# RWKV slots moved and the 16x16 inversion rewritten in a hybrid recurrent decoder layer

## The chip, the cores and the metric

One core of a Trainium2 chip runs the whole step. The metric is device time in microseconds (us), as the median of several executions. The engines are TensorE (PE in the profile), VectorE (DVE), ScalarE (ACT), GpSimd (POOL) and the DMA queue of SyncE (SP); each works through its own queue of instructions in order, and they meet at semaphores.

## The reference, cut to what matters

One layer with three parallel branches (HGRN2, RWKV-7, a short gated convolution) on 256 prompt tokens and 8 x 8 sample tokens, merged by sigmoid gates, then an MLP. The change touches the RWKV branch alone. Per head (16 heads of 64 channels), token after token:

```python
def step(S, inp):                       # S: [value, key]
    r_, w_, k_, v_, kk_, a_ = inp
    sa = jnp.einsum('bhij,bhj->bhi', S, -kk_)
    S = (S * w_[:, :, None, :] + sa[..., None] * (kk_ * a_)[:, :, None, :]
         + v_[..., None] * k_[:, :, None, :])
    return S, jnp.einsum('bhij,bhj->bhi', S, r_)
...
o_rw = (o_rw + bonus.reshape(Bn, T, RW_WIDTH)) * g      # after a group norm; g = sigmoid(gd) @ rw_g2
y_b = o_rw @ w_pb
```

The kernel does this in chunks of 64 tokens (four of the prompt, one that holds the 64 sample tokens). Within a chunk the tokens depend on one another through a strictly triangular 64x64 matrix N per head, and the kernel needs the inverse of (1 - N).

## The kernel before, in words

**Stages.** First a short prologue (about 30 us), then the RWKV stage with the convolution (about 30 to 545 us), then HGRN2 with the first merge, two more merges, the output projection, and the MLP. Each large product is split into two float32r parts, three matmuls for one: a weight granule `raw` of 128x1024 comes by DMA (line 128), ScalarE rounds it to `whi_t` (line 120), VectorE writes the rest `wlo_t` (line 121), and TensorE runs lines 147 to 149.

**Slots.** The order of TensorE's queue in the RWKV stage is written out by hand: a loop over slots, and in each some steps of dense projections (8 of 128x320 for each granule), with steps of the five chains `front`, `sample`, `chunk`, `solve` and `tail` between them. Heads go in pairs, eight pairs (0 to 7), 12 slots apart. A tuple says in which slots after its start a pair's chain makes its next step: `FRONT = (-7, -6, -3, 0, 1, 2)`, `SOLVE = (0, 2, 9, 15, ...)`, `CHUNK = 21 to 32`, `TAIL = (33, 39, 40)`. The other engines' queues are put in order by a scheduler with its own estimate of time and by priorities, so a change of cost or place there moves other instructions too.

**A pair's way.** The dense steps give its tiles k, r and v; `shift_mix` mixes each with the token before (POOL: `Rk` or `Rr`, then `Rd` at line 351; DVE: `xsk`, `xsr`, `xsv` at line 353).

- `front` step 1: squares on ScalarE (466), sums on TensorE (469), a reciprocal root. Step 2: two small products `lora` (489), ScalarE's sigmoids and exponential, POOL's `sg` (499), DVE's scan `Wp` (501), `W`, and its reciprocal `Wi` (505). Step 3: transposes (512), then `kkn` (516), `LYR` (522, 523 on DVE, 524, 525 on POOL), `a` times `Wi` on POOL (530), and `BK` (529, 531 on DVE, 532 on ScalarE).
- `solve` step 1 (line 592): products of `BK` and `LYR` into `pi`, masked into `Nb`. Step 2: the sample chunk's; then `Nb` goes to DRAM (616), its forty diagonal 16x16 blocks (five chunks, two heads, four each) come back as 40 partitions of 256 numbers, `Nd` (621), are inverted into `Pd`, are stored (649), and the whole comes back as `Pm` (651). From slot 15 on TensorE joins the 16x16 inverses to 32 and 64 (672 to 685).
- `chunk`: per chunk of 64 tokens three steps, each of them a product that needs what the step before left in `X` or `Y` (line 730 and, for the sample, 785 copy `X` on DVE; 725 makes `Sw` on POOL).
- `tail`: group norm, and as its last step the gate product (848) and its use (850).

**The inversion before**, all on VectorE: inside each 4x4 block by substitution (lines 631, 633), then twice joined, 4 to 8 and 8 to 16, by products that are written out as a multiplication into `t1` (638) and a sum over it (640).

Of the kernel before, what the change touches and what calls it, by code (L numbers as in the profile page):

```python
# [9 lines left out]
F32 = mybir.dt.float32  # L10
# [3 lines left out]
ALU = mybir.AluOpType  # L14
# [76 lines left out]
NSLOT = 12  # L91
URGENT = 1000

FRONT = (-7, -6, -3, 0, 1, 2)
SOLVE = (0, 2, 9, 15, 16, 17, 18, 19, 20)
SAMPLE = (20, 21, 22, 23)

CONV = (3, 0, 1, 1, 1, 1, 1, 0)
CHUNK = tuple(range(21, 33))
TAIL = (33, 39, 40)  # L100


class K:
# [252 lines left out]
    def rwkv(self, cx):  # L356
# [43 lines left out]
        blocks = (50 - len(self.early)) * 16  # L400
        chains = ((front, FRONT), (sample, SAMPLE), (chunk, CHUNK), (solve, SOLVE), (tail, TAIL))
        total = 8 * NSLOT + TAIL[-1] + 1
        with self.tc.manual_schedule(engines={mybir.EngineType.PE}):
# [168 lines left out]
    def rwkv_solve(self, j, wp):  # L572
        nc, io = self.nc, self.io
        V, G, S, T = nc.vector, nc.gpsimd, nc.scalar, nc.tensor
# [8 lines left out]
        for mk, cc in (("mkp", slice(0, 4)), ("mks", slice(4, 5))):  # L583
            n = cc.stop - cc.start
# [9 lines left out]
            for h, rows in ((0, lo), (1, hi)):  # L594
# [4 lines left out]
                m = self.cst(mk)  # L599
# [11 lines left out]
        def blocks(d, c):  # L611
            v = d.rearrange("(b w) -> b w", w=_DG)[:, 0:16 * 640]
            return v.rearrange("b (s x) -> b s x", x=640)[:, :, c * 128:c * 128 + 16]
        dN, dP = self.dN[j % 2], self.dP[j % 2]
        flat = lambda d: d[0:128 * 640].rearrange("(p x) -> p x", x=640)
        nc.sync.dma_start(flat(dN), Z["Nb%d" % (j % 2)])
        Nf = wp.tile([40, 272], F32, name="Nd")
        Pf = wp.tile([40, 272], F32, name="Pd")
        Nd, Pd = (t[:, 0:256].rearrange("p (s t) -> p s t", t=16) for t in (Nf, Pf))
        for c in range(5):  # L620
            nc.sync.dma_start(Nd[8 * c:8 * c + 8], blocks(dN, c))
        S.copy(Pf[:, 0:256], self.cst("eye16")[0:40])

        dg = lambda t: t.rearrange("p (b x) -> p b x", x=68)[:, :, 0:64].rearrange(
            "p b (s t) -> p b s t", t=16)[:, :, :, 0:4]
        N4, P4 = dg(Nf), dg(Pf)
        t1 = wp.tile([40, 512], F32, name="t1")
        for u in (3, 2, 1):
            w = 4 - u
            t4 = t1[:, 0:4 * u * w].rearrange("p (b s t) -> p b s t", b=4, t=w)  # L630
            V.tensor_mul(t4, N4[:, :, 0:u, u:u + 1].to_broadcast([40, 4, u, w]),
                         P4[:, :, u:u + 1, u:4].to_broadcast([40, 4, u, w]))
            V.tensor_add(P4[:, :, 0:u, u:4], P4[:, :, 0:u, u:4], t4)

        def product(out, x, y, n):

            t3 = t1[:, 0:n * n * n].rearrange("p (s t u) -> p s t u", t=n, u=n)
            V.tensor_mul(t3, x.unsqueeze(2).to_broadcast([40, n, n, n]),
                         y.rearrange("p u t -> p t u").unsqueeze(1).to_broadcast([40, n, n, n]))
            V.tensor_reduce(out, t3, axis=mybir.AxisListType.X, op=ALU.add)  # L640
        np_ = wp.tile([40, 64], F32, name="np")
        for n in (4, 8):
            for o in range(0, 16, 2 * n):
                a, b = slice(o, o + n), slice(o + n, o + 2 * n)
                m = np_[:, 0:n * n].rearrange("p (s t) -> p s t", t=n)
                product(m, Nd[:, a, b], Pd[:, b, b], n)
                product(Pd[:, a, b], Pd[:, a, a], m, n)
        for c in range(5):
            nc.sync.dma_start(blocks(dP, c), Pd[8 * c:8 * c + 8])
        yield  # L650
# [755 lines left out]
```

## Time and profile before

| | |
|---|---|
| median of 3 runs | 2437.85 us (2435.94 to 2445.15) |
| profiled execution | 2436.21 us, span 2434.4 us |
| busy: PE, PEld, DVE, ACT, POOL | 98%, 95%, 59%, 39%, 15% |
| mean granted TensorE clock | 0.993 |
| RWKV stage, 180 to 240 us (60 us): PE, DVE, ACT, POOL busy | 57.42, 54.66, 31.02, 17.83 us |
| MLP, 1600 to 2380 us (780 us): PE, DVE, ACT, POOL busy | 780.00, 391.89, 264.90, 7.94 us |

The span runs from the first to the last instruction of one execution. Matmuls are pipelined, so a busy PE is not PE at its peak. In the MLP TensorE never waits; in the RWKV stage it does, and VectorE is nearly as busy as it is. A row of a timeline is: start, duration, engine, line, operation, tiles written and read, shape, and in brackets the idle time of the engine before it with what ended that.

### The profile page before, as it was taken

The numbers are of one execution on the slowest core, as the hardware profiler recorded it, in microseconds if no ns is written. First come the engines' busy times: TensorE is split into PE (matmuls) and PEld (weight loads), VectorE is DVE, ScalarE is ACT, GpSimd is POOL, SyncE is SP. The second block draws the span as 40 slices with busy tenths as digits, with TensorE's granted clock in tenths as the row PEclk, the third lists the DMA queues.
The fourth block names the chain that finished last, engine by engine and source line by source line (L and its number), as shares of the span: only waits on it lengthen the run. The fifth ranks groups of instructions, "written<-read, shape, count | busy, mean of one in ns | idle before, by whom it ended". The sixth has DMA issues, their size and how long they took to land.

```text
span 2434.4 us, 40742 instructions
## 1 busy us (share of the span) xinstructions
PE 2384.3 (98%) x16190; PEld 2317.6 (95%) x16190; DVE 1441.4 (59%) x2485; ACT 961.3 (39%) x1467; POOL 362.1 (15%) x494
## 2 busy tenths in 40 slices
PE   8899999999999999999999999999999999999998
PEld 8899998999999999999999897999999999999996
DVE  6879898666566555644555336644555545554545
ACT  6445444334444444433433335333333333333333
POOL 4423332121111111100000442200000000000003
PEclk9999999999999999999999999999999999999999
DMA  6433434345434443444444744444444444444443
GB/s 224 121 122 113 112 124 129 124 141 183 138 137 140 141 141 127 144 150 147 150 154 147 246 177 153 153 153 151 147 150 153 147 149 152 150 147 152 152 147 130
DMA packets 136877, 360.23 MB, mean 148 GB/s; under 512 B 35440, under 2 KB 48112, under 8 KB 136688
## 3 DMA queue, kind: packets, MB, share of 16 engines
q1 hardware_dynamic: 136688, 357.63, 43.2%
q8 instruction: 128, 2.10, 0.3%
q14 instruction: 61, 0.50, 0.1%
HBM read 339.82 MB, written 17.76 MB: 147 GB/s over the span
## 4 chain that ended last, share of the span: by engine, by line
PE 89%; DVE 6%; ACT 2%; POOL 1%; issue 1%; DMA 1%; SPq 0%; DVEq 0%; POOLq 0%; ACTq 0%
PE mm_t L147 27%; PE mm_t L148 27%; PE mm_t L149 26%; DVE wlo_t L121 1%; PE plv_t L1025 1%; PE pho_t L1075 1%; ACT whi_t L120 1%; PE pi L677 1%; PE pi L592 0%; PE pi L684 0%; PE wide_t L1146 0%; PE wide_t L1147 0%; PE wide_t L866 0%; DVE m L1333 0%; DVE Wi L505 0%
## 5 line engine op out<-in xcount | busy, mean ns | idle before, releaser
L120 ACT CAST whi_t<-raw 128x1024 fp32r<-128x1024 f32 (+1 forms) x600 | 625.2, 1043 | 1137.2 <-PE mm_t L148 984.3
L121 DVE TENSOR_TENSOR wlo_t<-raw,whi_t 128x1024 fp32r<-128x1024 f32 (+1 forms) x600 | 764.8, 1276 | 433.3 <-ACT whi_t L120 431.9
L147 PE MATMUL mm_t<-xh,whi_t 128*128 128x320 f32 x2048 | 648.7, 317 | 0.0
L148 PE MATMUL mm_t<-xl,whi_t 128*128 128x320 f32 x2048 | 635.5, 310 | 0.0
L149 PE MATMUL mm_t<-xh,wlo_t 128*128 128x320 f32 x2048 | 634.8, 310 | 0.0
L147 PEld LDWEIGHTS mm_t<-xh,whi_t 128*128 128x128 f32 x2048 | 386.2, 189 | 7.6 <-issue 4.0
L148 PEld LDWEIGHTS mm_t<-xl,whi_t 128*128 128x128 f32 x2048 | 386.4, 189 | 1.1
L149 PEld LDWEIGHTS mm_t<-xh,wlo_t 128*128 128x128 f32 x2048 | 385.9, 188 | 0.0
L147 PE MATMUL mm_t<-hh,whi_t 128*128 128x320 f32 x1232 | 381.1, 309 | 0.0
L149 PE MATMUL mm_t<-hh,wlo_t 128*128 128x320 f32 x1232 | 380.4, 309 | 0.0
L148 PE MATMUL mm_t<-hl,whi_t 128*128 128x320 f32 x1232 | 380.4, 309 | 0.0
L147 PE MATMUL mm_t<-rh,whi_t 128*128 128x320 f32 x1024 | 316.4, 309 | 0.0
L149 PE MATMUL mm_t<-rh,wlo_t 128*128 128x320 f32 x1024 | 316.4, 309 | 0.0
L148 PE MATMUL mm_t<-rl,whi_t 128*128 128x320 f32 x1024 | 316.4, 309 | 0.0
L147 PEld LDWEIGHTS mm_t<-hh,whi_t 128*128 128x128 f32 x1232 | 231.1, 188 | 6.5 <-ACT whi_t L120 6.5
L148 PEld LDWEIGHTS mm_t<-hl,whi_t 128*128 128x128 f32 x1232 | 231.1, 188 | 0.0
L149 PEld LDWEIGHTS mm_t<-hh,wlo_t 128*128 128x128 f32 x1232 | 231.1, 188 | 0.0
L147 PEld LDWEIGHTS mm_t<-rh,whi_t 128*128 128x128 f32 x1024 | 192.2, 188 | 0.0
L148 PEld LDWEIGHTS mm_t<-rl,whi_t 128*128 128x128 f32 x1024 | 192.2, 188 | 0.0
L149 PEld LDWEIGHTS mm_t<-rh,wlo_t 128*128 128x128 f32 x1024 | 192.2, 188 | 0.0
L1308 DVE TENSOR_TENSOR m<-m,mm_t 128x320 f32<-128x320 f32 x112 | 54.6, 487 | 152.3 <-PE mm_t L149 152.3
L1238 POOL TENSOR_TENSOR ssf<-ssf,sqt 128x320 f32<-128x320 f32 x14 | 19.5, 1396 | 834.8 <-ACT sqt L1237 834.8
(423 smaller groups left out, 2716.7 us busy)
## 6 DMA issues: line engine op xcount, KB each, us to landing
raw<-w_in SPq DMA_DIRECT2D x256, 512.0 KB
raw<-w_ff SPq DMA_DIRECT2D x256, 512.0 KB
raw<-w_o SPq DMA_DIRECT2D x32, 512.0 KB
hs<-s_hg SPq DMA_DIRECT2D x16, 512.0 KB
raw<-w_pc SPq DMA_DIRECT2D x16, 512.0 KB
raw<-w_pb SPq DMA_DIRECT2D x16, 512.0 KB
raw<-w_pa SPq DMA_DIRECT2D x16, 512.0 KB
o_hgs<-hsn SPq DMA_DIRECT2D x16, 256.0 KB
```

The lines of the kernel that those rows point to most:

```text
L120: self.nc.scalar.copy(hi, src)
L121: self.nc.vector.tensor_sub(lo, src, hi)
L147: mmul(ps[:, :NT], hi[:, w], ah[:, i, :], start=(i == 0), stop=False)
L148: mmul(ps[:, :NT], hi[:, w], al[:, i, :], start=False, stop=False)
L149: mmul(ps[:, :NT], lo[:, w], ah[:, i, :], start=False, stop=(i == n - 1))
L677: T.matmul(ps[:, half(i)], Nb[:, i, :], cols(Mm[:, i, :], h, 0), start=True, stop=True)
L1025: T.matmul(ps[:, 0:128], KM, rh[:, 0:2 * hb], start=True, stop=True)
L1075: T.matmul(op[:, 256:320], s0[:, b, :], QX[:, 64 * b:64 * b + 64], start=(b == 0), stop=False)
L1238: (nc.vector if last else nc.gpsimd).tensor_add(acc, acc, t)
L1308: nc.vector.tensor_add(d, d, ps)
```

## The change

Two edits of tuples and one of code. The first three steps of a pair's front are taken one slot earlier against its solve; the last step of the tail, the gate product, two slots later (the stage gets 139 slots for 137). The inversion of the 16x16 blocks becomes one substitution over all 16 rows, 15 times a multiplication into `t1` and an addition into `Pd`, on GpSimd; step u has u x (16 - u) elements on 40 partitions. The tiles lose their padding, and `t1` is taken anew in each step.

```diff
-FRONT = (-7, -6, -3, 0, 1, 2)
+FRONT = (-8, -7, -4, 0, 1, 2)
 SOLVE = (0, 2, 9, 15, 16, 17, 18, 19, 20)
...
-TAIL = (33, 39, 40)
+TAIL = (33, 39, 42)
...
-        for u in (3, 2, 1):
-            w = 4 - u
-            t4 = t1[:, 0:4 * u * w].rearrange("p (b s t) -> p b s t", b=4, t=w)
-            V.tensor_mul(t4, N4[:, :, 0:u, u:u + 1].to_broadcast([40, 4, u, w]),
-                         P4[:, :, u:u + 1, u:4].to_broadcast([40, 4, u, w]))
-            V.tensor_add(P4[:, :, 0:u, u:4], P4[:, :, 0:u, u:4], t4)
-
-        def product(out, x, y, n):
-
-            t3 = t1[:, 0:n * n * n].rearrange("p (s t u) -> p s t u", t=n, u=n)
-            V.tensor_mul(t3, x.unsqueeze(2).to_broadcast([40, n, n, n]),
-                         y.rearrange("p u t -> p t u").unsqueeze(1).to_broadcast([40, n, n, n]))
-            V.tensor_reduce(out, t3, axis=mybir.AxisListType.X, op=ALU.add)
-        np_ = wp.tile([40, 64], F32, name="np")
-        for n in (4, 8):
-            for o in range(0, 16, 2 * n):
-                a, b = slice(o, o + n), slice(o + n, o + 2 * n)
-                m = np_[:, 0:n * n].rearrange("p (s t) -> p s t", t=n)
-                product(m, Nd[:, a, b], Pd[:, b, b], n)
-                product(Pd[:, a, b], Pd[:, a, a], m, n)
+        for u in range(15, 0, -1):
+            w = 16 - u
+            t1 = wp.tile([40, 16, 16], F32, name="t1")
+            G.tensor_mul(t1[:, 0:u, 0:w], Nd[:, 0:u, u:u + 1].to_broadcast([40, u, w]),
+                         Pd[:, u:u + 1, u:16].to_broadcast([40, u, w]))
+            G.tensor_add(Pd[:, 0:u, u:16], Pd[:, 0:u, u:16], t1[:, 0:u, 0:w])
```

Line numbers above 624 are 20 smaller in the changed kernel (730 becomes 710, 785 becomes 765, 616 stays).

What the scheduler makes of it, on POOL, in the front of pair 3, during which pair 2 is inverted. Before:

```order
L499 TENSOR_TENSOR sg<-wt,c 128x320
L348 COPY Rk<-Rk 128x31
L349 COPY shl<-Rk 128x9
L351 TENSOR_TENSOR Rd<-Rk 128x320
L551 MEMSET X 64x64
```

Now, from the second LYR of pair 3 to the v tile's mix, with the last of pair 2's substitution steps (L625 multiplies, L627 adds) between:

```order
L525 TENSOR_TENSOR LYR<-W,xsr 64x5x64
L627 TENSOR_TENSOR Pd<-Pd,t_2078 40x3x13
L494 COPY wt<-zero 128x1
L625 TENSOR_TENSOR t_2081<-Nd,Pd 40x2x14
L627 TENSOR_TENSOR Pd<-Pd,t_2081 40x2x14
L625 TENSOR_TENSOR t_2084<-Nd,Pd 40x15
L627 TENSOR_TENSOR Pd<-Pd,t_2084 40x15
L530 TENSOR_TENSOR a<-a,Wi 128x320
L348 COPY Rk<-Rk 128x31
L349 COPY shl<-Rk 128x9
L351 TENSOR_TENSOR Rd<-Rk 128x320
```

The v tile's Rd, which stood right behind sg, stands now behind all thirty steps and behind a. On DVE at the same place, before (gs and otm are the group norm of an earlier pair, Ms and T steps of sample and solve):

```order
L501 SCALAR_TENSOR_TENSOR Wp<-sg,c 128x320
L353 SCALAR_TENSOR_TENSOR xsv<-Rd,p,Rk 128x320
L503 TENSOR_TENSOR W<-Wp,wt 128x320
L812 TENSOR_REDUCE gs<-otm 128x5
L505 RECIPROCAL Wi<-W 128x320
L121 TENSOR_TENSOR wlo_t<-raw,whi_t 128x1024
L813 TENSOR_SCALAR gs<-gs 128x5
L516 SCALAR_TENSOR_TENSOR kkn<-xsk,p,pa_t 128x320
L815 TENSOR_TENSOR otm<-otm,gs 128x320
L785 COPY X<-pa_t 64x64
L730 COPY X<-py_t 64x64
```

And now:

```order
L353 SCALAR_TENSOR_TENSOR xsv<-Rd,p,Rk 128x320
L516 SCALAR_TENSOR_TENSOR kkn<-xsk,p,pa_t 128x320
L529 TENSOR_TENSOR BK<-tk,Wi 128x5x64
L522 TENSOR_TENSOR LYR<-Wp,kkn 64x5x64
L523 TENSOR_TENSOR LYR<-Wp,kkn 64x5x64
L531 SCALAR_TENSOR_TENSOR BK<-kkn,a 128x5x64
L792 TENSOR_REDUCE gs<-otm 128x5
L793 TENSOR_SCALAR gs<-gs 128x5
L795 TENSOR_TENSOR otm<-otm,gs 128x320
L121 TENSOR_TENSOR wlo_t<-raw,whi_t 128x1024
L765 COPY X<-pa_t 64x64
L710 COPY X<-py_t 64x64
```

The copies of X, which stood ahead of BK, stand behind xsv, all of BK and a weight split. On SP, from the store of pair 2's blocks, before:

```order
L616 DMA dN_424<-Nb_402 128x640
L621 DMA Nd<-dN_424 8x16x16
L128 DMA raw<-w_in 128x1024
L621 DMA Nd<-dN_424 8x16x16 x4
L128 DMA raw<-w_in 128x1024
L461 DMA lw<-lw 128x128
L128 DMA raw<-w_in 128x1024
L649 DMA dP_426<-Pd 8x16x16 x2
```

And now:

```order
L616 DMA dN_424<-Nb_402 128x640
L620 DMA Nd<-dN_424 8x16x16 x2
L128 DMA raw<-w_in 128x1024
L620 DMA Nd<-dN_424 8x16x16 x3
L461 DMA lw<-lw 128x128
L128 DMA raw<-w_in 128x1024
L775 DMA dX_325<-W 128x8x1
L629 DMA dP_426<-Pd 8x16x16 x3
```

One weight load fewer stands between the arrival of the blocks and the first store of the inverse.

More of the change, by code (lines that the diff above doesn't have):

```diff
@@ L616, in rwkv_solve @@
         nc.sync.dma_start(flat(dN), Z["Nb%d" % (j % 2)])
-        Nf = wp.tile([40, 272], F32, name="Nd")
-        Pf = wp.tile([40, 272], F32, name="Pd")
-        Nd, Pd = (t[:, 0:256].rearrange("p (s t) -> p s t", t=16) for t in (Nf, Pf))
+        Nd = wp.tile([40, 16, 16], F32, name="Nd")
+        Pd = wp.tile([40, 16, 16], F32, name="Pd")
         for c in range(5):
             nc.sync.dma_start(Nd[8 * c:8 * c + 8], blocks(dN, c))
[L622 to L627, printed above, removed]
-        for u in (3, 2, 1):
-            w = 4 - u
-            t4 = t1[:, 0:4 * u * w].rearrange("p (b s t) -> p b s t", b=4, t=w)
-            V.tensor_mul(t4, N4[:, :, 0:u, u:u + 1].to_broadcast([40, 4, u, w]),
-                         P4[:, :, u:u + 1, u:4].to_broadcast([40, 4, u, w]))
-            V.tensor_add(P4[:, :, 0:u, u:4], P4[:, :, 0:u, u:4], t4)
-        def product(out, x, y, n):
-            t3 = t1[:, 0:n * n * n].rearrange("p (s t u) -> p s t u", t=n, u=n)
-            V.tensor_mul(t3, x.unsqueeze(2).to_broadcast([40, n, n, n]),
-                         y.rearrange("p u t -> p t u").unsqueeze(1).to_broadcast([40, n, n, n]))
-            V.tensor_reduce(out, t3, axis=mybir.AxisListType.X, op=ALU.add)
-        np_ = wp.tile([40, 64], F32, name="np")
-        for n in (4, 8):
-            for o in range(0, 16, 2 * n):
-                a, b = slice(o, o + n), slice(o + n, o + 2 * n)
-                m = np_[:, 0:n * n].rearrange("p (s t) -> p s t", t=n)
-                product(m, Nd[:, a, b], Pd[:, b, b], n)
-                product(Pd[:, a, b], Pd[:, a, a], m, n)
+        S.copy(Pd.rearrange("p s t -> p (s t)"), self.cst("eye16")[0:40])
+        for u in range(15, 0, -1):
[4 more added lines that the diff above has]
+            G.tensor_add(Pd[:, 0:u, u:16], Pd[:, 0:u, u:16], t1[:, 0:u, 0:w])
         for c in range(5):
```

## The prediction

> **What bounds the kernel.** I read the page's first part, then the waits of TensorE between 30 and 545 us (the RWKV stage, the only one that the change touches), then the timeline around those waits on all engines.
>
> ```profile
> PE 2384.3 (98%) x16190; PEld 2317.6 (95%) x16190; DVE 1441.4 (59%) x2485; ACT 961.3 (39%) x1467; POOL 362.1 (15%) x494
> ...
> PE pi L592 <- DVE BK L531: 11.0, 3, 4.3
> PE pi L592 <- DVE BK L529: 3.6, 3, 2.1
> PE pa_t L566 <- ACT BT L568: 2.8, 2, 2.3
> PE pa_t L848 <- DVE o L844: 2.5, 1, 2.5
> PE py_t L733 <- DVE X L730: 2.3, 2, 1.9
> PE pi L592 <- ACT BK L532: 0.8, 1, 0.8
> ```
>
> TensorE is the bound: 50 us of the span are not matmul. A wait row gives total us, times, longest. In the RWKV stage TensorE mostly waits at L592, the first product of a pair's solve, for BK, the last result of that pair's front: 11.0 + 3.6 + 0.8 = 15.4 us. The gate product L848 waits once, 2.5 us; the chunk product L733 waits for DVE's copies of X, 2.3 us. Time is lost after a wait too:
>
> ```profile
> 72.00:80.00 8.00, 7.07 (x41) 0.79 0.25 87
> 112.00:120.00 8.00, 6.26 (x33) 0.57 0.33 102
> 160.00:168.00 8.00, 5.27 (x31) 0.79 0.37 116
> 208.00:216.00 8.00, 5.93 (x51) 1.00 0.43 163
> ```
>
> The fourth column is the granted clock of 8 us around the waits of pairs 0 to 3. Those of 3.3 to 4.3 us lost 8 x 0.21, 8 x 0.43 and 8 x 0.21 = 6.8 us of full-speed time; the one of 2.07 us lost none. So 15.4 + 2.5 + 2.3 + 6.8 = 27.0 us is what the change can reach.
>
> ```profile
> 94.30 0.16 DVE L631 TENSOR_TENSOR t<-Nd,Pd 40x12 f32<-40x12 f32 x1
> 113.74 1.59 PE L592 MATMUL pi<-LYR,BK 64*128 64x128 f32 x8 [4.30 <-DVE BK L531]
> 138.64 0.16 DVE L631 TENSOR_TENSOR t<-Nd,Pd 40x12 f32<-40x12 f32 x1 [1.72 <-DMA Nd<-dN]
> 155.21 0.39 PE L733 MATMUL py_t<-X,BT 128*128 128x128 f32 x2
> 162.63 1.78 PE L592 MATMUL pi<-LYR,BK 64*128 64x128 f32 x11 [3.41 <-DVE BK L531]
> 183.89 0.97 POOL L725 TENSOR_SCALAR Sw<-X,W 64x64 f32<-64x64 f32 x2 [1.37 <-DVE X L739]
> 206.09 0.39 PE L733 MATMUL py_t<-X,BT 128*128 128x128 f32 x2
> 382.47 0.97 POOL L725 TENSOR_SCALAR Sw<-X,W 64x64 f32<-64x64 f32 x2 [5.78 <-DVE X L739]
> 404.75 0.39 PE L733 MATMUL py_t<-X,BT 128*128 128x128 f32 x2
> ```
>
> A slot is (162.63 - 3.41 - 113.74) / 12 = 3.8 us. The blocks to invert are there at 94.3 for pair 0 and at 138.6 for pair 1. For pairs 2 to 6 (first and last shown) the new order of POOL puts Sw ahead of the inversion: it starts at 184.9 to 383.4.
>
> **The change, part by part.**
>
> *Inversion leaves DVE.* Busy time of the instructions that touch Pd, and the one group beside them:
>
> ```profile
> 30.00:545.00 515.00, 43.13 (x120) 0.99 0.40 125
> L640 DVE TENSOR_REDUCE np<-t 40x16 f32<-40x64 f32 (+1 forms) x24 | 8.7, 362 | 0.4
> ```
>
> (43.1 + 8.7) / 8 = 6.5 us of DVE per pair go. I count no gain for them: in the new DVE order L353 xsv, the end of the v tile's mix, stands ahead of the rest of the front, and it waits for POOL's Rd, which stands behind the whole inversion. DVE idles there instead.
>
> *POOL's turn: 30 substitution steps, and what stands between and behind them (sg, two LYR, wt, a, then the v tile's three).* No row shows a 40-partition product on POOL. Nearest rows, min/median/max ns:
>
> ```profile
> L915 POOL TENSOR_TENSOR sb<-sb,cv x8: 311/804/1488, 71.1 to 546.6; 128x64 f32<-128x64 f32 x8
> L349 POOL COPY shl<-Rr x8: 189/194/203, 43.4 to 375.8; 128x9 f32<-128x9 f32 x8
> L351 POOL TENSOR_TENSOR Rd<-Rr x8: 720/722/1780, 48.7 to 376.0; 128x320 f32<-128x320 f32 x8
> L499 POOL TENSOR_TENSOR sg<-wt,c x8: 874/1068/1415, 59.5 to 391.7; 128x320 f32<-128x320 f32 x8
> L530 POOL TENSOR_TENSOR a<-a,Wi x8: 867/1390/3315, 66.3 to 405.1; 128x320 f32<-128x320 f32 x8
> 148.66 0.85 POOL L524 TENSOR_TENSOR LYR<-W,xsr 64x320 f32<-64x320 f32 x1 [1.03 <-DVE W L503]
> 149.58 0.87 POOL L525 TENSOR_TENSOR LYR<-W,xsr 64x320 f32<-64x320 f32 x1
> ```
>
> Few elements take 0.19 us, 64 undisturbed 0.31: 0.19 + 0.0019 per element. Steps have u x (16 - u) elements, 45 on average: 0.275 us. Each waits for the one before it; L525, waiting for L524 on the same engine, starts 0.07 late. 30 x 0.345 = 10.4 us. The rest: 0.87 + 0.85 + 0.87 + 0.19 + 0.87 + three of the v tile at 0.24, 0.19, 0.72 = 4.8. Sum 15.2 us undisturbed. It will not be undisturbed:
>
> ```profile
> 581.06 1.38 POOL L1073 COPY QX<-QP 128x64 f32<-128x64 f32 x1 [14.81 <-DVE KS L1050]
> 581.12 1.21 DVE L121 TENSOR_TENSOR wlo_t<-raw,whi_t 128x1024 fp32r<-128x1024 f32 x1
> L121 DVE TENSOR_TENSOR wlo_t<-raw,whi_t 128x1024 fp32r<-128x1024 f32 x95 | 124.6, 1312 | 27.3 <-ACT whi_t L120 26.5 <-DMA Nd<-dN 0.4
> ```
>
> A 64-element copy on POOL lasts as long as the weight split on DVE that began beside it. Splits take 124.6 of 515 us, 24%. If each holds POOL, the turn is 15.2 / 0.76 = 20.0 us; a held step hides its fixed part, so I take **19 us**, bounds 15.2 (nothing held) and 24 (the rival below).
>
> *Who waits for the turn.* Behind it DVE has xsv, kkn, BK, two LYR, BK: six at about 0.5 us, as here; then a split, and four copies of X.
>
> ```profile
> 202.38 0.54 DVE L516 SCALAR_TENSOR_TENSOR kkn<-xsk,p,pa_t 128x320 f32<-128x320 f32 x1
> 207.63 0.48 DVE L522 TENSOR_TENSOR LYR<-Wp,kkn 64x320 f32<-64x320 f32 x1
> 203.38 0.22 DVE L785 COPY X<-pa_t 64x64 f32<-64x64 f32 x1
> ```
>
> Pair 1 (no chunks run yet): TensorE is at L592 at 113.74 - 4.30 = 109.4; six steps, a split inside and ACT's copy of BK take 4.7; budget of the turn 109.4 - 94.3 - 4.7 = 10.4 us, short by 8.6. Pair 2: the X copies, before in front of kkn, now stand behind BK, and L733 needs them at 155.2, one slot ahead of L592: 155.2 - 138.6 - (3.0 + 1.2 + 0.9) = 11.5, short by 7.5. Pairs 3 to 7 have three small otm steps (1.1) more: 206.1 - 184.9 - 6.2 = 15.0, and 404.75 - 383.4 - 6.2 = 15.1 for the last: short by 4.0 each. Sum 8.6 + 7.5 + 20 = 36.1 us. In before L733's 2.3 us show that a late X stops TensorE at once.
>
> *First steps one slot ahead.* Pair 0's squares end late as it is:
>
> ```profile
> 48.62 0.56 ACT L466 ACTIVATE sq<-xsk,p 128x320 f32<-128x320 f32 x1
> 50.07 0.72 PE L469 MATMUL pa_t<-c,sq 128*128 128x2 f32 x6
> ```
>
> One slot earlier TensorE asks at 46.3 and waits 2.9 us; its wait at L592 (3.34, in the 15.4) then goes. For later pairs the slot lets lora and kkn's transposes start 3.8 us earlier, which the turn swallows.
>
> *Gate product two slots behind.* The 2.5 us at L848 goes, since 7.6 us are added. The stage gets 139 slots for 137 with the same matmuls; the dense steps spread over two slots more. I cost it at nothing: the cover is the dense work that follows without a break.
>
> *SP.* The five stores of Pd now wait for POOL, with weight loads behind them, each up to a turn late.
>
> ```profile
> 183.63 0.36 SPq L128 DMA_DIRECT2D raw<-w_in  x1
> 198.48 1.05 ACT L120 CAST whi_t<-raw 128x1024 fp32r<-128x1024 f32 x1 [1.95 <-PE mm_t L148]
> ```
>
> The load issued at 183.6 is split at 198.5, and then because TensorE freed a buffer. Some 11 us late would still be in time; cost nothing, and if the cover goes, a few us per pair.
>
> *Sum.* Waits after: 36.1 + 2.9 = 39.0, clock after them: 3.4 each for pairs 1 and 2, 1.7 for each of the five of 4 us (between the 2.07 that lost nothing and the 4.30 that lost 3.4) = 15.3. Before: 20.2 and 6.8. Net 54.3 - 27.0 = **+27 us**. The profiled execution took 2436.21 us (span 2434.4), 1.6 below the median of 2437.85; 2436.2 + 27 = 2463 us.
>
> A page speaks on the clock: the Trainium skill, "TensorE: Matmul & The Clock Gate", Part 1, puts TensorE at half clock after an idle window of about 3.4 us. The rows agree roughly (3.34 us already lost some). By it the waits of 4 us would lose up to 3.4 each, which makes the sum some 8 us larger.
>
> **Rivals.**
>
> *Faster: the turn is short.* If held steps cost nothing and the turn is 15.2 us, pairs 3 to 7 are in time, pairs 1 and 2 are short by 4.8 and 3.7, pair 0 by 2.9: 11.4 + 5.1 of clock against 27.0, -10.5 us: 2426. Place L592, where BK comes in time. For it: DVE loses 6.5 us of work per pair, and the front starts a slot earlier. Against: the 24% of splits. It decides below 15.5 us.
>
> *No change: the turn is about 16.5 us.* At 16.5 waits are 6.1 + 5.0 + 7.5 + 2.9 = 21.5 and clock 6: the 27 us are lost elsewhere than now. 2437 us, decided between 15.5 and 17.6.
>
> *Much slower: POOL's products cost far more.* With steps at twice DVE's (0.16 to 0.22 in the rows above, so about 0.4) the turn is 30 x 0.125 longer undisturbed, 19.0, held 24: short by 13.6, 12.5 and five times 9: 71 + 2.9 + 24 of clock - 27 = +71: 2507 us. For it: no POOL row shows so small a product with one input broadcast and the other strided. Against: POOL's Rd takes 0.72 where DVE's kkn of one size takes 0.54. The rule behind it: the Trainium skill, "GPSIMD Engine Reference", section 4.1, says elementwise work belongs on VectorE, GpSimd being about twice slower for two inputs; by the row the factor is 1.3.
>
> **How the numbers follow.** Forecast 0.44, the faster case 0.18, no change 0.20, much slower 0.18. 2463 is the likeliest. The range, 2424 to 2494, takes in the faster case's 2426 and a turn up to 22 us (+57 us), leaving out about 0.2 in all; the forecast's own range, turns of 17.6 to 22, is 2448 to 2494. A change of 0.5% is 12 us, about what a measurement can tell: faster 0.18, same 0.20, slower 0.62.
>
> **What would show it.** On POOL 30 steps with starts about 0.35 us apart, longer where a split runs; from the first to the v tile's Rd 19 us. DVE idle some 5 us before xsv, ended by POOL. TensorE: L592's waits small for pairs 3 to 7, but waits at the product of L733 and at its neighbour for X, near 4 us each; near 8 us for pairs 1 and 2; L848's gone. Wrong if steps start under 0.25 us apart, if xsv is never waited for, or if weight splits wait for their load.

## Result and profile after

| | before | after |
|---|---|---|
| median, 4 runs each | 2441.5 us (2435.94 to 2447.55) | 2475.44 us (2473.63 to 2476.88) |
| ratio | 1 | 1.0139 (95%: 1.0118 to 1.0161) |
| span of the profiled execution | 2434.4 us | 2475.1 us |
| mean granted TensorE clock | 0.993 | 0.981 |

The kernel is slower by 34 us in the medians and 41 us between the two profiled executions (that of before was among its fastest). The page's busy row:

```profile
PE 2403.4 (97%) x16190; PEld 2336.2 (94%) x16190; DVE 1406.0 (57%) x2341; ACT 961.4 (39%) x1467; POOL 434.8 (18%) x734
```

The waits of TensorE, and two of VectorE (DVE), from 30 to 590 us: total us, times, longest. Lines above 624 are 20 smaller than before.

```profile
PE py_t L713 <- DVE X L710: 30.8, 5, 7.3
PE pa_t L544 <- DVE xsv L353: 4.6, 1, 4.6
PE pi L664 <- DVE T L660: 2.9, 1, 2.9
PE pi L592 <- DVE BK L531: 2.8, 1, 2.8
PE pa_t L763 <- ACT Y L760: 2.0, 1, 2.0
PE pa_t L469 <- POOL Rk L345: 1.8, 1, 1.8
PE pa_t L769 <- DVE X L765: 1.6, 1, 1.6
PE pi L652 <- issue: 0.9, 1, 0.9
...
DVE Wp L501 <- POOL sg L499: 37.5, 8, 8.1
DVE xsv L353 <- POOL Rd L351: 12.1, 3, 6.2
```

DVE has 35 us less to do and POOL 73 us more, and TensorE waits longer. The 15.4 us at L592 and the 2.5 us at the gate product are gone but for 2.8; in their place TensorE stops five times at L713, once for each of pairs 3 to 7. DVE's wait at Wp for sg took next to nothing before (1.6 us); now it is 37.5 us. The timelines at pair 4 of DVE, TensorE and POOL (of POOL the first and last of the thirty steps, sg with the step ahead of it, and the v tile's Rd):

```profile
251.40 0.92 DVE L501 TENSOR_TENSOR_SCAN Wp<-sg,c 128x320 f32<-128x320 f32 x1 [5.45 <-POOL sg L499]
...
255.01 1.70 DVE L121 TENSOR_TENSOR wlo_t<-raw,whi_t 128x1024 fp32r<-128x1024 f32 x1
256.64 0.45 DVE L710 COPY X<-py_t 64x64 f32<-64x64 f32 x2
...
257.24 0.77 PE L713 MATMUL py_t<-X,BT 128*128 128x128 f32 x2 [5.43 <-DVE X L710]
...
244.03 0.47 POOL L625 TENSOR_TENSOR t<-Nd,Pd 40x15 f32<-40x15 f32 x1
...
250.23 0.30 POOL L625 TENSOR_TENSOR t<-Nd,Pd 40x63 f32<-40x63 f32 x1
250.49 0.87 POOL L499 TENSOR_TENSOR sg<-wt,c 128x320 f32<-128x320 f32 x1
...
259.91 0.21 POOL L627 TENSOR_TENSOR Pd<-Pd,t 40x15 f32<-40x15 f32 x1
...
261.31 0.71 POOL L351 TENSOR_TENSOR Rd<-Rk 128x320 f32<-128x320 f32 x1
```

Read upward from TensorE, against the order of time: L713 starts at 257.24 because X was copied at 256.64; the copies stand in DVE's queue behind Wp, W, Wi and a weight split; Wp waited 5.45 us for sg; sg stood on POOL behind seventeen of the thirty steps. The rest of the turn, to the v tile's Rd at 262.0, is 18.0 us in all, and at this pair DVE does not wait for its end.

The granted clock (fourth column) in 16 us from about the ends of those five stops, then in 8 us around the stops of pairs 1 and 2:

```profile
201.00:217.00 16.00, 15.21 (x81) 0.68 0.38 117
257.00:273.00 16.00, 15.76 (x88) 0.72 0.38 120
314.00:330.00 16.00, 15.53 (x83) 0.69 0.43 131
372.00:388.00 16.00, 15.77 (x84) 0.69 0.58 144
428.00:444.00 16.00, 15.97 (x90) 0.73 0.57 152
...
112.00:120.00 8.00, 5.16 (x29) 0.57 0.63 212
148.00:156.00 8.00, 6.76 (x39) 0.79 0.01 3
```

The five cost 16 x 0.32, 0.28, 0.31, 0.31 and 0.27: 5.1, 4.5, 5.0, 5.0 and 4.3 us, 23.8 together; with 3.4 and 1.7 for pairs 1 and 2 it is 28.9 us, against 6.8 before.

### The profile page after: what moved, and what is told of

It is laid out like the page before. It is cut to its first block, busy times and chain, and to the rows that moved or that the text cites. A ratio compares the mean times of both kernels' runs of the same rounds, so it can differ in the third digit from the quotient of the medians.

```text
span 2475.1 us, 40851 instructions
## 1 busy us (share of the span) xinstructions
PE 2403.4 (97%) x16190; PEld 2336.2 (94%) x16190; DVE 1406.0 (57%) x2341; ACT 961.4 (39%) x1467; POOL 434.8 (18%) x734
## 4 chain that ended last, share of the span: by engine, by line
PE 88%; POOL 4%; DVE 3%; issue 2%; DMA 1%; ACT 1%; SPq 0%; POOLq 0%; DVEq 0%; ACTq 0%
PE mm_t L147 27%; PE mm_t L148 26%; PE mm_t L149 26%; POOL Pd L627 1%; POOL t L625 1%; DVE wlo_t L121 1%; PE plv_t L1005 1%; PE pho_t L1055 1%; ACT whi_t L120 1%; PE wide_t L1126 0%; PE pi L664 0%; PE wide_t L1127 0%; PE pi L592 0%; PE wide_t L846 0%; DVE m L1313 0%
```

## Experiments

Theory A at the start was the prediction's: POOL's long turn holds DVE in order, DVE's late X stops TensorE, and its clock halves. Ratios are to the kernel before, on the same chip.

**The two halves apart.** e1 is the changed kernel with the old tuples; e2 is the kernel before with the new ones.

```diff
 # e1, from the changed kernel
-FRONT = (-8, -7, -4, 0, 1, 2)
-TAIL = (33, 39, 42)
+FRONT = (-7, -6, -3, 0, 1, 2)
+TAIL = (33, 39, 40)
```

> The substitution on GpSimd with the old slots (front -7, -6, -3 and gate product at 40). Theory A (GpSimd's turn of about 18 us holds VectorE at Wp and xsv; X comes late; TensorE stops at L713 and its clock halves behind each stop): the turn stays about 18 us, but with the old slots the scheduler puts the X copies ahead of BK, so the stops move from L713 to L592, 2440 to 2465 us. Rival B (the moved slots carry the loss): about 2440 or below. Rival D (the turn's length alone counts, in whatever order VectorE's work stands): 2475 us or more, since the front then starts a slot later.

> The new slots with the old inversion on VectorE. Theory A: L592's 15.4 us, the gate product's 2.5 and the 6.8 us of clock mostly go, up to 2.9 us at L469 and as much clock come: 2415 to 2435 us. Rival B (the moved slots carry the loss): near the changed kernel's 2475, about 2470 us, with the stops at L713 still there.

e1: 2461.08 us, 1.0075 (1.0052 to 1.0097). e2: 2429.52 us, 0.9948 (0.9927 to 0.9968). TensorE's three longest waits in e1:

```profile
PE py_t L713 <- DVE X L710: 10.9, 3, 5.9
PE pa_t L758 <- DVE Ms L753: 10.6, 4, 4.5
PE pi L592 <- DVE BK L531: 9.3, 2, 6.5
```

And two of e2 (with the line numbers of before):

```profile
PE pi L672 <- DMA Pm<-dP: 5.3, 1, 5.3
...
PE pi L592 <- DVE BK L531: 3.3, 1, 3.3
```

So the slots are not the loss (rival B falls), they gain 0.5%; the inversion costs 0.75% alone, and e1 stays below rival D's 2475 us. The effects don't add: 0.75 less 0.5 is not 1.39. e1's time is in theory A's range, but its stops are not where that put them: of the 30.8 us in the three rows of e1 only 9.3 are at L592. In e2 pair 1's 3.3 us is all that is left at L592.

**The engine or the form of the inversion.** e4: the thirty steps on VectorE.

```diff
-            G.tensor_mul(t1[:, 0:u, 0:w], ...
+            V.tensor_mul(t1[:, 0:u, 0:w], ...
-            G.tensor_add(Pd[:, 0:u, u:16], ...
+            V.tensor_add(Pd[:, 0:u, u:16], ...
```

> The changed kernel with its thirty substitution steps on VectorE, slots new. Theory A (the engine matters, not the form of the inversion): VectorE has 30 x about 0.2 = 6 us for the 6.5 us of before, GpSimd's turn is gone: 2415 to 2435 us, as with the slots alone. Rival E (the chain of thirty dependent steps is what is long, on any engine): VectorE's queue is held by 8 us or more per pair, stops at L713 or L592 remain: 2455 us or more.

2436.65 us, 0.9989 (0.9975 to 1.0004); L713's waits are 7.4 us in five, none above 2.0. On DVE the 240 steps take 27.76 + 25.81 us, 6.7 per pair; on POOL, after the change, 10.4 per pair:

```profile
30.00:545.00 515.00, 83.14 (x240) 0.93 0.36 113
```

Theory A's upper bound is missed by 2 us, rival E falls: on DVE the chain of thirty steps takes about as long as the old inversion (6.5 us by the prediction's working), so the engine matters. Beside e2 the form costs some 0.4%.

**POOL's other work moved away.** e3 gives `sg`, `a` times `Wi` and the v tile's last steps to DVE, which then waits for none of POOL's turn.

```diff
-        nc.gpsimd.tensor_sub(d, R[:, :, 0:8], R[:, :, 1:9])
+        (nc.vector if name == "v" else nc.gpsimd).tensor_sub(d, R[:, :, 0:8], R[:, :, 1:9])
-        G.tensor_mul(ws, wt[:, :NT], self.cst("m01"))
+        V.tensor_mul(ws, wt[:, :NT], self.cst("m01"))
-        G.tensor_mul(a, a, Wi)
+        V.tensor_mul(a, a, Wi)
```

> The changed kernel, but sg (L499), a times Wi (L530) and the v tile's shift and Rd (L348, L351) on VectorE; the thirty substitution steps stay on GpSimd. Theory A: VectorE no longer waits for the turn at Wp, xsv or BK; the stops at L713 go although the steps still take 10 us or more: 2415 to 2440 us. Rival C (the stores and weight loads queued on SP behind the late Pd make TensorE late): nothing changes there, 2465 us or more. Rival D (VectorE is short of time altogether): four more instructions of about 0.6 us each for VectorE, 2465 us or more.

2469.36 us, 1.0107 (1.0083 to 1.0131): theory A missed, and by the time alone rivals C and D would fit; the waits tell more. L713's 30.8 us are gone (0.9 left), but others stand there: L763 for ScalarE's Y 24.1 us, L699 for X 12.8. ScalarE (ACT) now has a long wait of its own (two more at the same line, of 10.6 and 13.8 us, stand under other transfers):

```profile
ACT Pd L621 <- DMA dP<-Pd: 42.4, 4, 13.2
```

Its timeline near 320 us, and what TensorE and DVE wait for there:

```profile
319.79 0.40 ACT L621 COPY Pd<-c 40x256 f32<-40x256 f32 x1 [13.19 <-DMA dP<-Pd]
320.22 0.42 ACT L760 COPY Y<-pa_t 64x64 f32<-64x64 f32 x2
...
321.13 1.04 ACT L120 CAST whi_t<-raw 128x1024 fp32r<-128x1024 f32 x1
...
320.69 0.69 PE L763 MATMUL pa_t<-Y,Pm 128*128 128x64 f32 x2 [7.49 <-ACT Y L760]
...
322.20 1.23 DVE L121 TENSOR_TENSOR wlo_t<-raw,whi_t 128x1024 fp32r<-128x1024 f32 x1 [10.43 <-ACT whi_t L120]
```

The identity that starts the next pair's Pd (L621) needs the buffer that the last pair's store still reads. It stands in ACT's queue ahead of Y and of the rounding of weights, and so the turn's end holds ACT. After the change the same copy waits for the stores 5.4 us in all; there ACT waits for TensorE instead (39.7 us at L725, for the product behind L713).

**Two buffers for Pd.** e5 adds them to e3, e6 to the changed kernel.

```diff
-        Pd = wp.tile([40, 16, 16], F32, name="Pd")
+        Pd = wp.tile([40, 16, 16], F32, name="Pd%d" % (j % 2))
```

> The kernel with sg, a times Wi and the v tile's last steps on VectorE, and with two buffers for Pd in turn, so that the identity copy (L621) in ScalarE's queue no longer waits for the store of the pair before. In the run with the first part alone ScalarE idled up to 13.2 us at L621, seven times, and held Y and the rounding of weights. Theory A (the turn's end reaches TensorE through queues that wait for it in order: VectorE's, and with that mended ScalarE's): with both mended TensorE's stops go, 2415 to 2440 us, the thirty steps as long as before. Rival D (VectorE has too much work): 2460 us or more, with TensorE's stops ended by VectorE.

> The changed kernel with two buffers for Pd and nothing else. Theory A (in the changed kernel VectorE's waits for sg and Rd stop TensorE, ScalarE's L621 idles beside them): the stops at L713 stay, 2465 to 2478 us. Rival F (ScalarE's wait for the one Pd buffer is the cause all along): 2450 us or less.

e6: 2476.21 us, 1.0141 (1.0123 to 1.0159), L713's waits 30.5 us: ACT's wait is not what stops the changed kernel, rival F falls. e5: 2463.7 us, 1.0087 (1.0069 to 1.0106), a miss. (In e3's trace the waits at L621 that its expectation names are six, the longest 13.8 us.) The row `ACT Pd L621 <- DMA dP<-Pd` still has 40.3 us, the longest 14.0: with a second buffer the scheduler queues the copy one pair earlier, and it waits for the same store.

**Half the steps.** e7 leaves out every second step, so that the inverse is not formed.

```diff
-        for u in range(15, 0, -1):
+        for u in range(15, 0, -2):
```

> The changed kernel with every second step of the substitution left out, 16 instructions for 30 (the inverse is then not formed). VectorE's order around the front is that of the changed kernel. By the prediction's own working the turn falls from 18 to about 12.5 us, below its 15.5 us: Theory A: the waits at L713 for pairs 3 to 7 go or shrink below 1.5 us, pair 1 keeps some 2 us, 2420 to 2437 us. Rival G (the order behind the moved slots is what costs, whatever the length of the turn): L713's waits stay above 3 us each, 2455 us or more.

2459.34 us, 1.0072 (1.0051 to 1.0092): the prediction's working fails here. TensorE's and DVE's waits:

```profile
PE py_t L713 <- DVE X L710: 20.4, 5, 4.7
...
DVE Wp L501 <- POOL sg L499: 27.7, 8, 5.0
```

And POOL's timeline at pair 4:

```profile
237.83 0.47 POOL L625 TENSOR_TENSOR t<-Nd,Pd 40x15 f32<-40x15 f32 x1
...
243.63 0.21 POOL L627 TENSOR_TENSOR Pd<-Pd,t 40x15 f32<-40x15 f32 x1
243.81 0.88 POOL L499 TENSOR_TENSOR sg<-wt,c 128x320 f32<-128x320 f32 x1
```

All sixteen steps now stand ahead of sg and take as long there (6.0 us) as the seventeen did (6.5). DVE's waits at Wp for pairs 3 to 7 are 4.2, 5.0, 4.5, 3.8 and 3.4 us, TensorE's at L713 4.30, 4.31, 4.69, 3.73 and 3.39; after the change they are 4.4, 5.4, 7.1, 8.1, 5.5 and 5.22, 5.43, 7.17, 7.32, 5.69. Pair by pair they agree within 1 us. That formed theory A2: L713 waits for sg, not for the turn's end.

**sg alone to DVE.** e10 has only that line of e3.

> The changed kernel with sg (L499) alone on VectorE. In the changed kernel VectorE idles at Wp for sg by 4.4 to 8.1 us for pairs 3 to 7, and TensorE's waits at L713 are 5.2 to 7.3 us, pair by pair within 1 us of it; with half the steps 3.4 to 5.0 and 3.4 to 4.7. Theory A2 (the copies of X stand behind Wp, and what they wait for is sg; sg waits for the steps ahead of it): L713's waits fall below 1.5 us each. The steps still hold the v tile's Rd, so VectorE then waits at xsv some 5 us for it, and a part of the stop comes back one or two slots later, at L699 or L757, where the second copies of X stand behind BK: 2440 to 2470 us. Theory A as predicted (xsv and what stands behind it holds X, sg does not matter): L713's waits stay near 5 us, 2470 us or more.

2462.82 us, 1.0091 (1.0062 to 1.0119). L713's waits are 0.8 us in all, as A2 said; DVE now waits at xsv, where the prediction had put it, and the stops come back, for Y and for the second copies of X, at L763 and L769 (L699 or L757 had been expected):

```profile
DVE xsv L353 <- POOL Rd L351: 44.3, 8, 8.7
...
PE pa_t L763 <- ACT Y L760: 23.1, 4, 8.8
PE pa_t L769 <- DVE X L765: 6.2, 2, 3.2
```

**Nothing but SP waits for the steps.** e11 is e3 with Pd set up on POOL.

```diff
-        S.copy(Pd.rearrange("p s t -> p (s t)"), self.cst("eye16")[0:40])
+        pf = Pd.rearrange("p s t -> p (s t)")
+        G.tensor_scalar_mul(pf, Nd.rearrange("p s t -> p (s t)"), 0.0)
+        G.memset(pf[:, 0:256:17], 1.0)
```

> The changed kernel with sg, a times Wi and the v tile's last steps on VectorE, and Pd set up on GpSimd from Nd (zeros, then ones on the diagonal) in place of ScalarE's identity copy, which had taken the wait over and did so with two Pd buffers too, since it is queued a pair earlier then. Theory A2 (what stops TensorE is a queue that waits in order for the end of the steps, first VectorE's, then ScalarE's): with no queue but SP's waiting for the steps, TensorE's stops of 5 us and more between 190 and 450 us go, though the steps take 12 us and more as before: 2425 to 2445 us. Rival D (VectorE has too much work): stops remain, ended by VectorE after no wait for GpSimd or ScalarE, 2455 us or more. Rival C (SP's queue behind the late stores): weight splits wait for a load, 2455 us or more.

2442.78 us, 1.0007 (0.9993 to 1.0020): against the kernel before, nothing measurable is left of the 1.39%. That includes what the slots gain: by the ratios, beside e2, which has the same slots and the old inversion, some 0.6% is still lost, of 1.9% after the change. POOL has the same thirty steps, busy for 12.2 us per pair in place of 10.4, and DVE has four more instructions per pair. Together with e10 this shows the mechanism, queues that wait in order for work on POOL, and that neither the steps' length nor DVE's load (the two rivals called D) makes up most of the loss. The two longest stops that remain behind 200 us, 3.44 and 4.49 us at L701 (the L699 of the others), come, by the traces, from a third queue, SP's, which is what rival C named, at a smaller price. The row of those stops, and SP's own wait row:

```profile
PE py_t L701 <- DVE X L723: 11.3, 4, 4.5
...
SPq L631 <- POOL Pd L629: 62.2, 5, 14.0
```

The second of the stops in the timeline of SP, ACT and TensorE:

```profile
252.47 0.36 SPq L128 DMA_DIRECT2D raw<-w_in  x1
...
256.53 1.04 ACT L120 CAST whi_t<-raw 128x1024 fp32r<-128x1024 f32 x1 [6.66 <-DMA raw<-w_in]
...
259.49 0.77 PE L701 MATMUL py_t<-X,LYR 128*128 128x128 f32 x2 [4.49 <-DVE X L723]
```

The weight loads (the first is shown) stand behind the late stores of Pd, ACT waits for it, DVE's split for ACT, and X stands behind the split. No run takes these last waits away. (Pair 1's 6.9 us at L592 stays as well.)

**The slots one by one.** e9 is the changed kernel with `TAIL` back at 40; e12 and e13 are the kernel before with the new `FRONT` alone and the new `TAIL` alone.

> The changed kernel with the gate product back at 40. Before 2438, substitution on GpSimd alone 2461, slots alone 2430, all together 2475 us: together they cost some 22 us more than the sum of the parts. Theory A (the front a slot earlier meets the turn, the tail matters little): 2468 to 2485 us. Rival H (it is the moved tail): 2440 to 2455 us.

> The kernel before with the front's slots moved and nothing else (inversion on VectorE, gate product at 40). Both slot moves together gave 2429.5 us against 2438 of before. By the prediction's steps the front takes away L592's waits (15.4 us and most of the 6.8 of clock) for up to 2.9 at L469, the gate product only 2.5 us: the front carries nearly all of it, 2428 to 2434 us; L592's waits below 6 us in all. Rival: it is the gate product's place, 2436 to 2442 us here.

> The kernel before with the gate product two slots later and nothing else. By the prediction's steps its 2.5 us of wait at L848 goes and no other: 2434 to 2438 us, L592's waits near 15 us as before. Rival (the tail carries the gain of the slots): 2432 us or less.

e9: 2464.32 us, 1.0094 (1.0072 to 1.0115), between both expectations. L713's waits are 21.0 us in five, the longest 8.1: the tail's move adds to the loss beside the inversion; how was not tried further. e12: 2433.45 us, 0.9967 (0.9955 to 0.9979): the front takes L592's waits to 4.4 us. e13: 2440.62 us, 1.0002 (0.9992 to 1.0011): no gain, above the 2434 to 2438 us expected. L848's wait is gone, and L592's grew from 15.4 to 22.4 us:

```profile
PE pi L592 <- DVE BK L531: 9.5, 3, 5.5
PE pi L592 <- DVE BK L529: 4.6, 3, 2.1
PE pi L592 <- DVE gt L825: 4.5, 1, 4.5
PE pi L592 <- ACT BK L532: 3.8, 3, 2.2
```

The best version run is e2, both moves with the old inversion: it beats both kernels.

## Why the prediction was right, and where not

The direction and the engine were right: POOL's turn, DVE in order behind it, late X, the clock. The path from the turn to TensorE was wrong for five of the eight pairs, so that the time fell into the range is in part luck. Term by term:

- *Inversion leaves DVE, no gain*: right. DVE's busy time fell by 35 us (8 x 6.5 = 52 had been reckoned; the rest is not placed), and it waits 37.5 + 12.1 us for POOL.
- *POOL's turn 19 us*: 18.0 at pair 4, 17.6 to 18.0 in the fronts of pairs 1 to 7. The steps' mean is 83.14 / 240 = 0.35 us, splits included; 0.345 had been taken undisturbed and with the gaps.
- *Who waits for the turn*: the step that failed for pairs 3 to 7. It put DVE's wait at xsv and X behind BK, and reckoned 15.0 us of budget for the whole turn. But DVE waits at xsv for pairs 0 to 2 alone (0.7, 6.2 and 5.2 us), and the L713 that was priced, the last one ahead of L592 (at 273.32 us for pair 4), does not wait at all. The stop is at the L713 one chunk earlier (257.24 us): its X stands behind Wp, and Wp waits for sg inside the turn. That the two products share a line number, so that the forecast stops seem to be found, is luck. The place was wrong, and the size: 30.8 us for 20. e7 exposes it: by the budget half the steps cost nothing, and 20.4 us stayed. For pair 1 (8.6 forecast, 4.6 at L544 + 2.8 at L592 measured) the account held; pair 2 got 2.9 + 1.6 for 7.5.
- *Pair 0*: 1.8 us at L469 for 2.9.
- *Gate product*: its 2.5 us went, but e13 shows that this alone is worth nothing; DVE is late, and TensorE waits one step later.
- *SP nothing*: right here. ACT waits for a weight load twice, 6.8 us in all, and TensorE waits for a weight split only once, 0.2 us. "A few us per pair if the cover goes" happened in e11.
- *Clock*: the term most mis-sized, 15.3 forecast and 28.9 measured. 1.7 us per stop was taken between two rows of before; each stop here lost 4.3 to 5.1, and in e7 one of 3.73 us did too (below). The estimate of up to 3.4 us each, which the prediction set beside a rule of the Trainium skill, "TensorE: Matmul & The Clock Gate", Part 1, was nearer and still too small. That section of the Trainium skill also gives about 3.4 us of steady work until the full clock is back. Here TensorE was busy for 15 to 16 of the 16 us and lost 4.3 to 5.1, which at half clock is 8.6 to 10.2 us (at pair 4 the granted clock was 0.50 from 257 to 265 us and 0.94 in the next 8). The measurement decides.

Waits and clock after are 48.0 + 28.9 us, before 25.4 + 6.8 (with the small rows of both views that are not shown): 44.7 us more, where the span grew by 40.7. The windows count some idle time twice; the rest of those 4 us is not placed. The profile thus shows more than the forecast's +27, by the failed step and the clock term, less what pairs 0 to 2 did not take.

## What to carry to other kernels

Work handed to an idle engine delays what stands behind it in that engine's queue, and then what stands behind the waiter in every other queue; look for such waits queue by queue (here DVE's Wp, then xsv, then ACT's set-up copy, then SP's stores ahead of loads). When two forms of a change differ, find the instruction that the stopped engine needs and read upward through the queue of its producer: a budget for a whole block of work says little if the needed result is produced in its middle. A second buffer helps only if the scheduler does not use it to queue the same wait earlier.

## What the hardware showed unexpectedly

The clock lost behind a stop is not set by the stop's length alone. The 16 us behind stops of 4.30 and 3.73 us in e7:

```profile
195.00:211.00 16.00, 15.77 (x82) 0.68 0.44 115
359.00:375.00 16.00, 15.47 (x82) 0.68 0.60 157
```

And behind stops of 6.31 and 8.85 us in e10:

```profile
314.00:330.00 16.00, 15.13 (x97) 0.81 0.47 156
372.00:388.00 16.00, 15.68 (x99) 0.81 0.33 115
```

The short ones lost 5.1 us each, the long ones 3.0. For the stop of 8.85 us the trace shows a part of the reason: from 368 to 372 us the granted clock is 0.50 already, while TensorE still stands, and a low clock costs nothing there. It is not all: after the change the clock is 0.50 from 370 to 372 us too, inside the stop of 7.32 us, and 5.0 us were lost behind it. The short ones stand at L713, ahead of the small products L748 and L664, the long ones at L763, ahead of dense steps after two small products; whether the kind of products is the cause was not tried.

On POOL a product or sum over 40 partitions took 0.21 us with 15 elements and 0.31 with 64 where nothing disturbed it; on DVE, in e4, the median multiplication took 0.20.
